# Weight loads two groups ahead instead of three, and sum loads half an interval sooner, in a hybrid attention and linear-attention block on Trainium2

## The chip, the core and the metric

The kernel runs on one core of one Trainium2 chip. The core's engines have queues of their own: TensorE (PE) multiplies matrices, VectorE (DVE) and ScalarE (ACT) work on rows of elements, GpSimd (POOL) helps, and SyncE (SP) issues most DMA transfers. Each queue runs in order. A queue stops at an instruction whose inputs, or whose target buffer, are not ready, and everything behind it stops too.

The metric is the device time of one execution in microseconds (us).

## The reference

The block takes 512 positions of width 2048. It normalises the input, projects it by one wide matrix, sends parts of the result through two token mixers, gates both with SiLU, and projects back:

```python
mod = jax.nn.silu(c) @ w_cond[layer] + b_cond[layer]
shift, scale, gate = jnp.split(mod, 3, axis=-1)
h = rms_norm(x) * (1.0 + scale[:, None]) + shift[:, None]
proj = h @ w_in[layer]
aq, ak, av, ag, gq, gk, gv, gg, lr_f, lr_b = jnp.split(proj, PROJ_SPLITS, axis=-1)
...                      # 16 attention heads over aq, ak, av (three dilated windows)
a_out = att.reshape(B, S, ATT_WIDTH) * jax.nn.silu(ag)
...                      # 4 heads of gated linear attention (GLA) over gq, gk, gv, both directions
g_out = g_o * jax.nn.silu(gg)
y = jnp.concatenate([a_out, g_out], axis=-1) @ w_out[layer]
x = x + gate[:, None] * y
return rms_norm(x) * final_gain
```

Two small products matter here. The row `shift` times the value columns of the weights gives a bias of the values, and `silu(c)` times the last third of `w_cond` gives the output gate. Both are a vector times a matrix, so the kernel doesn't use TensorE for them: VectorE multiplies a block of transposed weights by the row and adds up along it. These are the *sums* of this document.

## The kernel before

**Units.** The wide projection is worked in units of 512 columns: qk2, qk4, qk6, gk, gv0, gv1, ag0, ag1, gg0, gg1 (after two larger stages that don't matter here), and then the output projection. A unit has 8 groups of weights. A group is 256 input rows by 512 columns, 512 KB, loaded by one DMA into a raw buffer. Float32 accuracy comes from splitting: ACT rounds the group to a high part (`split_hi`, L442 in the profile), DVE subtracts that from the raw numbers to get a low part (`split_lo`, L428), and PE makes three products for each one (`three`, L215 to L217). So a group is 24 matmuls of 128x512.

**The ring of raw buffers.** There are four raw buffers of 512 KB (tag `raw`). The groups of weights (named `raw_ag13` for group 3 of unit ag1), the blocks for sums of values (`rawv`) and the blocks for sums of gates (`rawg`) share them. SP issues a load when the buffer's former owner has been read. A value sum (`bias_half`) has a load at L838 and an operation on DVE at L843 or L314; a gate sum (`gate_half`) has its load at L804 and its operation at L314, behind which stands a short read of the accumulator. In the names `rawv40` and `rawg91` the last digit is the half and the rest the number of the column block.

**What runs beside the matmuls.** PE's order is that of the program. In `unit`, after each pair of matmul triples a counter `tick` goes on by one, 64 in all, and side work whose time (a share of the unit) has come is issued there. In qk2 to gk it is attention: per head and window the logits `s` (L730, L731), the maximum and subtraction `p` on DVE (L734), the exponential on ACT, the transposes `t` (L754), their eviction `pt`, the product `o` (L768) and its combination `cat` (L775). In gv1 to gg0 it is GLA, one head per unit: gates `z` (L869) and their decays, `ki` (L898) and its transposes `kt` (L908), states, the masked product `at` (L954), the outputs `go`, their squares `gsq` and `gsl` (L974, L982), a matmul `gn` for the norm (L983, L984), and the normalised result `cat` (L992). Three PSUM banks serve this side work, so that z of the next head waits until L992 of the head before has read its bank.

**What sets the order.** `SUMS_IN` gives the number of sums of each unit (the rest are in gg1). `some_sums` gives each sum q of n two times in the unit: one for its load, (q − 0.3)/n, and one for its operation, (q + 0.7)/n. PE's order follows from the ticks. On the other engines a scheduler sets the order, from the priorities that this order of the program gives and from its own idea of when inputs are there. Gate sums are also held behind the last masking step of GLA (`masked`, L954). Loads of output weights and their combinations on POOL's queue (`T`, L391) are paced by ACT's `split_hi`.

Weights: `unit` fetches, for each group, the groups two and three ahead before it makes the low part of its own; `split_hi` of the next group fetches that, if it isn't fetched yet.

Of the kernel before, what the change touches and what calls it, by code (L numbers as in the profile page):

```python
# [114 lines left out]
SUMS_IN = {"qk6": 4, "gk": 4, "gv0": 9, "gv1": 2, "ag0": 7, "ag1": 9, "gg0": 9}  # L115
# [63 lines left out]
def block_kernel(ctx: ExitStack, tc: tile.TileContext, a: dict):  # L179
# [19 lines left out]
    def PJ(name):  # L199
        return pp.tile([P, 512], F32, tag="pj", bufs=5, name=name)  # L200
# [13 lines left out]
    def three(ps, lh, ll, rh, rl, first, last, more=False):  # L214
        mm(ps, lh, rh, start=first, stop=False, skip_group_check=more)  # L215
        mm(ps, ll, rh, start=False, stop=False, skip_group_check=more)  # L216
        mm(ps, lh, rl, start=False, stop=last, skip_group_check=more)  # L217
# [134 lines left out]
    def fetch(i):  # L352
        if i < len(groups) and i not in raws:
            u, g = groups[i]
            if u == "O":
                raws[i] = out_fetch(g)
            else:
                raws[i] = RAW(f"raw_{u}{g}", [2, 512])
                nc.sync.dma_start(raws[i], a["w_" + u][g])
# [54 lines left out]
    def block_sums(name):  # L414
        n = SUM_OPS_IN[name]
        r = [sum_ops.pop(0) for _ in range(n)]
        return [((q + 0.5) / n, x) for q, x in enumerate(r)]
# [5 lines left out]
    def split_lo(i):  # L423
        if i in raws and i not in low:
            u, g = groups[i]
            raw = raws[i].rearrange("p k c -> p (k c)")
            hi, lo = wts[i]
            tt(lo, raw, hi.bitcast(F32), op=ALU.subtract)  # L428
            low.add(i)

    def split_hi(i):
        if i < len(groups) and i not in wts:
            fetch(i)
            u, g = groups[i]
            raw = raws[i].rearrange("p k c -> p (k c)")
            dst = None
            if (u, g) == ("O", len(groups) - gi["O", 0] - 4):
                t = b8.tile([P, 2, 1024], F32R, tag="b8", name="wlast")
                dst = t[:, 0, :], t[:, 1, :]
            wts[i] = dst or (wp.tile([P, 1024], F32R, tag="whi", name=f"{u}{g}h"),  # L440
                             wp.tile([P, 1024], F32R, tag="wlo", name=f"{u}{g}l"))
            last["hi"] = act(wts[i][0], raw, AF.Copy).ins  # L442
# [177 lines left out]
    n = len(chain) // 2  # L620
# [4 lines left out]
    for z in range(2):  # L625
        for e in range(3):
            name = ("mm", "a", 0, 7) if (z, e) == (1, 2) else ("m0", z, e)
# [224 lines left out]
    def some_sums(name):  # L852
        r = [sum_work.pop(0) for _ in range(SUMS_IN.get(name, len(sum_work)))]
        n = len(r)
        loads = [(max(q - 0.3, 0.1) / n, x[0]) for q, x in enumerate(r)]
        return sorted(loads + [((q + 0.7) / n, x[1]) for q, x in enumerate(r)], key=lambda x: x[0])

    def gla_head(h):
# [142 lines left out]
    def urgent(go):  # L1001
        with tc.high_priority(offset=20):
            go()
# [3 lines left out]
    def unit(name, natural, side=(), lr=None):  # L1007
        side = sorted(spill + list(side) + block_sums(name), key=lambda x: x[0])
        spill[:] = [(at - 1, go) for at, go in side if at >= 1]
        side = [x for x in side if x[0] < 1]  # L1010
        ps = [PJ(f"ps_{name}_{i}") for i in range(4)]
        pos, tick, ticks = 0, 0, 64
        for g in range(KT // 2):
            i0 = gi[name, g]
            split_hi(i0)
            split_hi(i0 + 1)
            for ahead in (2, 3):
                fetch(i0 + ahead)
            split_lo(i0)
            hi, lo = wts[i0]  # L1020
            for i in range(4):
                for kk in range(2):
                    k = 2 * g + kk
                    rh, rl = h_hi[:, k, :], h_lo[:, k, :]
                    if natural:
                        t = slice(i * P, i * P + P)
                        cw = slice(kk * 512, kk * 512 + 512)
                        three(ps[i], rh[:, t], rl[:, t], hi[:, cw], lo[:, cw], k == 0, k == KT - 1)
                    else:
                        c = slice(kk * 512 + i * P, kk * 512 + i * P + P)  # L1030
                        three(ps[i], hi[:, c], lo[:, c], rh, rl, k == 0, k == KT - 1)
                    tick += 1
                    if tick % 8 == 2:
                        split_lo(i0 + 1)
                    while pos < len(side) and side[pos][0] * ticks <= tick:
                        urgent(side[pos][1])
                        pos += 1
                if lr is not None:
                    lr(4 * g + i)
        while pos < len(side):  # L1040
            urgent(side[pos][1])
            pos += 1
        return ps
# [14 lines left out]
    for n, p in (("qk2", 0), ("qk4", 2), ("qk6", 4)):  # L1058
        ps = unit(n, False, attention((p, p + 1)) + ([(0.05, shift_row)] + some_sums(n) if p == 4 else []))
        for q in range(2):  # L1060
            qk_evict(p + 2 + q, ps[2 * q], ps[2 * q + 1])

    ps = unit("gk", False, attention((6, 7)) + some_sums("gk"))
    gla["k"] = B8("gkt", [4, 512])
    for i in range(4):
# [12 lines left out]
    def lr_tick(n):  # L1078
        if n in at_tick:
# [3 lines left out]
            mm(plr[:64], w, h_lo[:, k, :], start=False, stop=k == KT - 1)  # L1083

    ps = unit("gv0", True, some_sums("gv0"), lr=lr_tick)
    gla["v0"] = B8("gv0", [4, 512])
    for i in range(4):
# [340 lines left out]
```

## Time and profile before

| | us |
|---|---|
| median of 3 runs | 942.91 (940.98 to 943.13) |
| the profiled execution | 940.34 |
| its span | 938.6 |
| PE busy in it | 917.5 (98%) |
| DVE busy | 654.6 (70%) |
| ACT busy | 472.2 (50%) |

The profile shows one execution, recorded by the hardware. Its span goes from the first to the last instruction, and times in its rows count from the span's start. A row of a timeline has the start, the duration, the engine, the line of the code, the operation, and the tiles with an arrow from inputs to output; in square brackets stands how long the engine stood idle before it and what ended that. Buffer numbers are left out in the profile's names, so `rawg` stands for all gate blocks. A row of a list of waits has the waiting engine, tile and line, an arrow to what it waited for, and then the sum in us, how many times, and the longest. A row of the list of DMA issues ends with the us from issue to landing. Matmul durations overlap, so their pace is read from start to start. The mean granted clock of TensorE in this execution was 0.994 of the full one.

### The profile page before, as it was taken

The numbers are of one execution on the slowest core, as the hardware profiler recorded it, in microseconds if no ns is written. First come the engines' busy times: TensorE is split into PE (matmuls) and PEld (weight loads), VectorE is DVE, ScalarE is ACT, GpSimd is POOL, SyncE is SP. The second block draws the span as 40 slices with busy tenths as digits, with TensorE's granted clock in tenths as the row PEclk, the third lists the DMA queues.
The fourth block names the chain that finished last, engine by engine and source line by source line (L and its number), as shares of the span: only waits on it lengthen the run. The fifth ranks groups of instructions, "written<-read, shape, count | busy, mean of one in ns | idle before, by whom it ended". The sixth has DMA issues, their size and how long they took to land.

```text
span 938.6 us, 12129 instructions
## 1 busy us (share of the span) xinstructions
PE 917.5 (98%) x4375; PEld 760.8 (81%) x4375; DVE 654.6 (70%) x960; ACT 472.2 (50%) x770; POOL 98.3 (10%) x152
## 2 busy tenths in 40 slices
PE   7999999999999999999999999989989999999996
PEld 6888888888888888888877888878878888888884
DVE  7988899766755676766444657476686639697496
ACT  5553533565655645655413545363643428555464
POOL 0000000012222122122000100111002000000001
PEclk9999999999999999999999999999999999999998
DMA  9999497465765775755656546666766567856743
GB/s 352 404 412 383 166 372 269 158 199 148 188 198 153 217 234 166 239 167 147 209 200 197 162 151 221 202 199 199 247 209 200 187 195 267 315 203 217 276 179 135
DMA packets 54339, 209.79 MB, mean 224 GB/s; under 512 B 7204, under 2 KB 7492, under 8 KB 45960
## 3 DMA queue, kind: packets, MB, share of 16 engines
q1 hardware_dynamic: 48656, 174.83, 51.1%
q0 software_dynamic: 5184, 33.62, 15.1%
q8 instruction: 34, 0.56, 0.2%
q10 hardware_dynamic: 440, 0.57, 0.2%
q14 instruction: 25, 0.20, 0.1%
HBM read 200.53 MB, written 37.83 MB: 254 GB/s over the span
## 4 chain that ended last, share of the span: by engine, by line
PE 81%; DMA 8%; DVE 7%; issue 3%; ACT 1%; POOL 0%; SPq 0%; DVEq 0%; POOLq 0%; ACTq 0%
DMA rawg<-in_wg 5%; PE ps_qk L215 4%; PE ps_qk L217 4%; PE ps_qk L216 4%; PE g L217 4%; PE g L215 4%; PE g L216 4%; PE stb L217 3%; PE stb L216 3%; PE stb L215 3%; PE o L768 3%; PE ps_gv L217 3%; PE ps_gv L216 3%; PE ps_gv L215 3%; PE t L754 3%
## 5 line engine op out<-in xcount | busy, mean ns | idle before, releaser
L737 ACT ACTIVATE p<-p,st 128x512 f32<-128x512 f32 x64 | 46.1, 720 | 56.3 <-DVE st L734 55.9
L314 DVE CUSTOM_DVE_ANT_0 cb<-cb,sb,c_bcond 128x2048 f32<-128x2048 f32 (+1 forms) x32 | 73.4, 2295 | 1.3 <-DMA cb<-in_wm 1.0
L391 POOL DMA_DIRECT2D T<-in_w_o x48 | 33.5, 704 | 311.3 <-ACT qk21h L442 119.8
L742 POOL TENSOR_SCALAR p<-p,st 128x512 f32<-128x512 f32 x62 | 43.2, 697 | 196.1 <-DVE st L738 152.9
L759 DVE TENSOR_TENSOR pt<-t,pt 128x512 fp32r<-128x512 f32 x64 | 43.7, 688 | 15.6 <-ACT pt L758 15.4
L734 DVE CUSTOM_DVE_ANT_0 p<-s,g 128x512 f32<-128x512 f32 x64 | 43.6, 686 | 13.7 <-PE s L731 13.4
L758 ACT ACTIVATE pt<-t 128x512 fp32r<-128x512 f32 x64 | 37.8, 591 | 9.9 <-PE t L754 8.9
L314 DVE CUSTOM_DVE_ANT_0 rawg<-rawg,sb,gate 128x1024 f32<-128x1024 f32 x16 | 20.5, 1283 | 31.1 <-DMA rawg<-in_wg 30.9
L754 PEld LDWEIGHTS t<-c_ident,p 128*128 128x128 f32 x256 | 31.5, 140 | 9.7 <-POOL p L742 1.4
L754 PE MATMUL t<-c_ident,p 128*128 128x128 f32 x256 | 38.5, 273 | 0.1
L768 PEld LDWEIGHTS o<-pt,vv 128*128 128x128 f32 x256 | 34.8, 188 | 2.8
L768 PE MATMUL o<-pt,vv 128*128 128x256 f32 x256 | 35.5, 281 | 0.0
L314 DVE CUSTOM_DVE_ANT_0 rawg<-rawg,sb,c_bcond 128x1024 f32<-128x1024 f32 x16 | 20.5, 1282 | 19.1 <-DMA rawg<-in_wg 19.0
L738 DVE RECIPROCAL st<-st 128x1 f32<-128x1 f32 x64 | 10.3, 161 | 24.9 <-ACT p L737 24.9
L730 PE MATMUL s<-ks,qs 128*128 128x512 f32 x64 | 25.1, 392 | 0.2 <-DVE cat L775 0.2
L731 PE MATMUL s<-kl,qs 128*128 128x512 f32 x64 | 25.0, 391 | 0.0
L937 ACT ACTIVATE sq<-st,sc 128x256 f32<-128x256 f32 x24 | 12.2, 508 | 22.1 <-DVE st L927 13.0
L843 DVE CUSTOM_DVE_ANT_0 rawv<-rawv,shb 128x1024 f32<-128x1024 f32 x8 | 9.8, 1225 | 16.0 <-DMA rawv<-in_wv 16.0
L314 DVE CUSTOM_DVE_ANT_0 rawv<-rawv,shb,vbias 128x1024 f32<-128x1024 f32 x8 | 10.3, 1282 | 15.0 <-DMA rawv<-in_wv 15.0
L1253 POOL TENSOR_SCALAR x<-x,rn 128x512 f32<-128x512 f32 x3 | 3.4, 1137 | 158.4 <-ACT rn L1242 158.4
L771 ACT ACTIVATE oh<-o 64x256 f32<-64x256 f32 x32 | 12.2, 382 | 13.7 <-PE o L768 12.7
L775 DVE TENSOR_TENSOR cat<-o,oh 64x256 f32<-64x256 f32 x32 | 13.3, 416 | 7.6 <-ACT oh L771 7.2
(1520 smaller groups left out, 2978.0 us busy)
## 6 DMA issues: line engine op xcount, KB each, us to landing
cb<-in_wm SPq DMA_DIRECT2D x31, 1024.0 KB, 8.5
T<-in_w_o POOLq DMA_DIRECT2D x48, 512.0 KB, 5.2
rawg<-in_wg SPq DMA_DIRECT2D x32, 512.0 KB, 4.6
raw_O<-T SPq DMA_DIRECT2D x32, 512.0 KB, 5.0
raw_qk<-in_w_qk SPq DMA_DIRECT2D x24, 512.0 KB, 3.3
raw_O<-in_w_o SPq DMA_DIRECT2D x24, 512.0 KB, 4.2
rawb<-in_w_sb SPq DMA_DIRECT2D x16, 512.0 KB, 4.9
T<-T POOLq DMA_DIRECT2D x16, 512.0 KB, 3.6
```

The lines of the kernel that those rows point to most:

```text
L215: mm(ps, lh, rh, start=first, stop=False, skip_group_check=more)
L216: mm(ps, ll, rh, start=False, stop=False, skip_group_check=more)
L217: mm(ps, lh, rl, start=False, stop=last, skip_group_check=more)
L314: nc.vector.tensor_tensor_reduce(out=w, in0=w, in1=with_, op0=ALU.mult, op1=ALU.add, scale=1.0, scalar=init, accum_out=dst)
L391: move = nc.gpsimd.dma_start(dst, src, max_dma_last_dim=8192, **how).ins
L734: nc.vector.tensor_tensor_reduce(out=t, in0=ps, in1=gt[h][:, P * i:P * i + 512], op0=ALU.add, op1=ALU.min, scale=1.0, scalar=3e38, accum_o ...
L737: act(t, t, AF.Exp, bias=st[:, 0:1], scale=-1.0, accum_out=st[:, 1:2])
L742: last["pool"] = nc.gpsimd.tensor_scalar(t, t, st[:, 2:3], 1.0, op0=ALU.mult, op1=ALU.mult).ins
L754: nc.tensor.transpose(pk[:, kt * P:kt * P + P], t[:, kt * P:kt * P + P], ident)
L758: act(hi, src, AF.Copy)
L759: tt(lo, src, hi.bitcast(F32), op=ALU.subtract)
L768: mm(po[:, :256], vv[h // 4][:, kt, h % 4, :], t[:, w, kt, :], start=kt == 0 and w == 0, stop=kt == 3 and w == 1)
```

## The change

In units that have sums (those in `SUMS_IN`, and gg1), `unit` fetches only the group two ahead. In all units, the load of a sum gets the time (q − 0.8)/n in place of (q − 0.3)/n, and at the least 0.05/n in place of 0.1/n; the times of the operations stay.

```diff
--- before.py
+++ after.py
@@ -852,7 +852,7 @@
     def some_sums(name):
         r = [sum_work.pop(0) for _ in range(SUMS_IN.get(name, len(sum_work)))]
         n = len(r)
-        loads = [(max(q - 0.3, 0.1) / n, x[0]) for q, x in enumerate(r)]
+        loads = [(max(q - 0.8, 0.05) / n, x[0]) for q, x in enumerate(r)]
         return sorted(loads + [((q + 0.7) / n, x[1]) for q, x in enumerate(r)], key=lambda x: x[0])
 
     def gla_head(h):
@@ -1014,7 +1014,7 @@
             i0 = gi[name, g]
             split_hi(i0)
             split_hi(i0 + 1)
-            for ahead in (2, 3):
+            for ahead in (2,) if name in SUMS_IN or name == "gg1" else (2, 3):
                 fetch(i0 + ahead)
             split_lo(i0)
             hi, lo = wts[i0]
```

No instruction is added or taken away. PE's and POOL's queues have the same order as before; on SP, DVE and in a few places on ACT the order is another. Three places follow. In all of them a name is the tile's with its number.

First, SP's queue at the end of unit gk, where the value sums of unit gv0 begin. Before:

```order
L359 DMA raw_gv03_4170<-in_w_gv0 128x1024
L838 DMA rawv40_4187<-in_wv 128x1024
L838 DMA rawv41_4202<-in_wv 128x1024
L359 DMA raw_gv04_4219<-in_w_gv0 128x1024
L838 DMA rawv50_4237<-in_wv 128x1024
L1070 DMA lrb_4157<-in_w_lr 128x512
L359 DMA raw_gv05_4252<-in_w_gv0 128x1024
L838 DMA rawv51_4269<-in_wv 128x1024
```

After, from the load of gv02 on:

```order
L359 DMA raw_gv02_4168<-in_w_gv0 128x1024
L838 DMA rawv40_4173<-in_wv 128x1024
L838 DMA rawv41_4191<-in_wv 128x1024
L359 DMA raw_gv03_4217<-in_w_gv0 128x1024
L838 DMA rawv50_4222<-in_wv 128x1024
L838 DMA rawv51_4247<-in_wv 128x1024
L359 DMA raw_gv04_4252<-in_w_gv0 128x1024
L838 DMA rawv60_4281<-in_wv 128x1024
```

The loads of sums 40 and 41 stand ahead of the load of gv03 rather than behind it, and that of sum 50 is right behind the load of gv03, with sum 51's behind it.

Second, DVE's queue at the end of GLA head 1, in unit ag0 and the first groups of ag1. Behind the masking step stand sums 31 and 40, and after the change also 41; then the rows go on. Before:

```order
L428 TENSOR_TENSOR ag10l_5302<-raw_ag10_5194,ag10h_5301 128x1024
L314 ISA rawg41_5289,gate_1489<-rawg41_5289,sb_89,gate0_1490 128x1024
L314 ISA gate_1489 128x1
L974 TENSOR_TENSOR gsq11_5271<-gsq11_5271,gsq10_5258 128x512
L982 TENSOR_TENSOR gsl1_5311<-gsq11_5271,gsh1_5310 128x512
L314 ISA rawg50_5393,gate0_1490<-rawg50_5393,sb_89,c_bcond_84 128x1024
L314 ISA gate0_1490 128x1
L428 TENSOR_TENSOR ag11l_5363<-raw_ag11_5242,ag11h_5362 128x1024
L314 ISA rawg51_5433,gate_1489<-rawg51_5433,sb_89,gate0_1490 128x1024
L314 ISA gate_1489 128x1
L992 TENSOR_SCALAR cat2_4893<-go10_5247,c_ggain_1487,gr1_5316 128x512
```

After:

```order
L428 TENSOR_TENSOR ag10l_5300<-raw_ag10_5242,ag10h_5299 128x1024
L314 ISA rawg50_5368,gate0_1490<-rawg50_5368,sb_89,c_bcond_84 128x1024
L314 ISA gate0_1490 128x1
L974 TENSOR_TENSOR gsq11_5271<-gsq11_5271,gsq10_5258 128x512
L314 ISA rawg51_5420,gate_1489<-rawg51_5420,sb_89,gate0_1490 128x1024
L314 ISA gate_1489 128x1
L982 TENSOR_TENSOR gsl1_5309<-gsq11_5271,gsh1_5308 128x512
L428 TENSOR_TENSOR ag11l_5361<-raw_ag11_5302,ag11h_5360 128x1024
L314 ISA rawg60_5451,gate0_1490<-rawg60_5451,sb_89,c_bcond_84 128x1024
L314 ISA gate0_1490 128x1
L992 TENSOR_SCALAR cat2_4891<-go10_5247,c_ggain_1487,gr1_5314 128x512
```

Ahead of `gsl1`, which PE's `gn` of head 1 needs, there stood one sum behind ag10's low part; now there are two others, 50 and 51, and a third, 41, stands ahead of it. Ahead of L992, for which z of head 2 waits, the last sum was 51 and is 60.

Third, DVE's queue at the same step of head 2, in the first groups of gg0. Before:

```order
L428 TENSOR_TENSOR gg00l_5746<-raw_gg00_5635,gg00h_5745 128x1024
L314 ISA rawg90_5739,gate0_1490<-rawg90_5739,sb_89,c_bcond_84 128x1024
L314 ISA gate0_1490 128x1
L974 TENSOR_TENSOR gsq21_5716<-gsq21_5716,gsq20_5703 128x512
L982 TENSOR_TENSOR gsl2_5755<-gsq21_5716,gsh2_5754 128x512
L314 ISA rawg91_5839,gate_1489<-rawg91_5839,sb_89,gate0_1490 128x1024
L314 ISA gate_1489 128x1
```

After:

```order
L428 TENSOR_TENSOR gg00l_5744<-raw_gg00_5685,gg00h_5743 128x1024
L314 ISA rawg91_5814,gate_1489<-rawg91_5814,sb_89,gate0_1490 128x1024
L314 ISA gate_1489 128x1
L974 TENSOR_TENSOR gsq21_5714<-gsq21_5714,gsq20_5701 128x512
L314 ISA rawg100_5866,gate0_1490<-rawg100_5866,sb_89,c_bcond_84 128x1024
L314 ISA gate0_1490 128x1
L982 TENSOR_TENSOR gsl2_5753<-gsq21_5714,gsh2_5752 128x512
```

Sums 91 and 100 moved ahead of `gsl2`; 90 stands further up. At head 3 one sum, 140, moved ahead of `gsl3` in the same way.

## The prediction

> **What bounds the kernel now.** I read the page's busy times and its chain of waits first, then the list of waits by engine, then the timeline around each wait that stops PE.
>
> ```profile
> PE 917.5 (98%) x4375; PEld 760.8 (81%) x4375; DVE 654.6 (70%) x960; ACT 472.2 (50%) x770; POOL 98.3 (10%) x152
> ...
> PE 81%; DMA 8%; DVE 7%; issue 3%; ACT 1%; POOL 0%; SPq 0%; DVEq 0%; POOLq 0%; ACTq 0%
> DMA rawg<-in_wg 5%; PE ps_qk L215 4%; PE ps_qk L217 4%; PE ps_qk L216 4%; PE g L217 4%; PE g L215 4%; PE g L216 4%; PE stb L217 3%; PE stb L216 3%; PE stb L215 3%; PE o L768 3%; PE ps_gv L217 3%; PE ps_gv L216 3%; PE ps_gv L215 3%; PE t L754 3%
> ```
>
> PE is busy 98% of the span, so matmul time bounds the kernel and the change touches none of it. What can move is PE's few waits. The chain gives 5% to loads of gate weights for sums, `rawg`, although no matmul reads them. PE's waits, then DVE's:
>
> ```profile
> PE kt L908 <- DVE ki L898: 3.1, 1, 3.1
> PE z L869 <- DVE cat L992: 2.9, 1, 2.9
> ...
> PE s L730 <- DVE cat L775: 0.2, 1, 0.2
> PE gn L984 <- DVE gsl L982: 0.2, 1, 0.2
> ```
>
> ```profile
> DVE rawg L314 <- DMA rawg<-in_wg: 50.0, 18, 5.7
> ```
>
> Four waits of PE lie in units with sums, and each is for DVE. DVE in turn stands 50.0 us before `rawg` sums. The two long PE waits and their aftermath on PE's timeline:
>
> ```profile
> 616.29 0.39 PE L216 MATMUL ps_ag<-h_hi,ag10l 128*128 128x512 f32 x1
> 616.52 0.39 PE L217 MATMUL ps_ag<-h_lo,ag10h 128*128 128x512 f32 x1
> 619.81 0.76 PE L869 MATMUL z<-lrst,ups 128*128 128x512 f32 x1 [2.90 <-DVE cat L992]
> 620.37 0.63 PE L215 MATMUL ps_ag<-h_hi,ag10h 128*128 128x512 f32 x1
> ...
> 622.92 0.39 PE L215 MATMUL ps_ag<-h_hi,ag10h 128*128 128x512 f32 x1
> ...
> 641.00 0.49 PE L908 MATMUL kt<-c_ident,ki 128*128 128x128 f32 x3
> ...
> 698.41 0.90 PE L908 MATMUL kt<-c_ident,ki 128*128 128x128 f32 x3 [3.14 <-DVE ki L898]
> ```
>
> Ahead of the wait matmuls start 0.23 us apart (616.29, 616.52). Behind it, from 620.37 to 622.92, six start 0.425 apart. So the z wait costs 2.9 us and about 1.3 of slow matmuls (z and six more, 0.2 each), 4.2 in all. The kt wait costs 3.1 and a slow restart (0.90 for three transposes against 0.49 at 641.00), which I put at 1. With the two waits of 0.2 some 8.7 us, say 9, is the most that this change can win. DVE ahead of the z wait:
>
> ```profile
> 596.14 0.69 DVE L954 SCALAR_TENSOR_TENSOR at<-c_ident,at 128x512 f32<-128x512 f32 x1
> ...
> 601.80 1.28 DVE L314 CUSTOM_DVE_ANT_0 rawg<-rawg,sb,gate 128x1024 f32<-128x1024 f32 x1
> ...
> 606.68 0.69 DVE L982 TENSOR_TENSOR gsl<-gsq,gsh 128x512 fp32r<-128x512 f32 x1 [0.70 <-ACT gsh L981]
> 610.57 1.28 DVE L314 CUSTOM_DVE_ANT_0 rawg<-rawg,sb,c_bcond 128x1024 f32<-128x1024 f32 x1 [3.19 <-DMA rawg<-in_wg]
> ...
> 617.71 1.28 DVE L314 CUSTOM_DVE_ANT_0 rawg<-rawg,sb,gate 128x1024 f32<-128x1024 f32 x1 [4.70 <-DMA rawg<-in_wg]
> 618.92 0.74 DVE L992 SCALAR_TENSOR_TENSOR cat<-go,c_ggain,gr 128x512 f32<-128x512 f32 x1
> ```
>
> L992, which PE wants, stands behind a sum that waits 4.70 us for its load. The load's row on SP's queue, and what loads took here and elsewhere (the first three from 512 KB issues in short windows, the last two over all loads of `rawg` and of `rawv`):
>
> ```profile
> 603.12 9.10 SPq L804 DMA_DIRECT2D rawg<-in_wg  x2
> ```
> ```profile
> rawg<-in_wg SPq DMA_DIRECT2D x1, 512.0 KB, 5.7
> ```
> ```profile
> T<-in_w_o POOLq DMA_DIRECT2D x1, 512.0 KB, 7.7
> ```
> ```profile
> raw_gv<-in_w_gv SPq DMA_DIRECT2D x1, 512.0 KB, 3.1
> ```
> ```profile
> DMA to landing us min/median/max: 3.1/4.6/7.3
> ```
> ```profile
> DMA to landing us min/median/max: 3.3/4.1/5.8
> ```
>
> The second load of the pair goes out at 611.9, when the sum that started at 610.57 has ended: both use the same buffer, since weights three groups ahead hold the other three. Load, sum, load, sum run in series, 5.7 + 1.3 us each.
>
> **The change part by part.** No instruction and no byte is added; PE's and POOL's orders stay. SP issues each sum's load about one place sooner and weights one group later, and DVE's queue gets sums ahead of work that stood before them. The last is what can cost.
>
> *Weights a group later.* A group is 24 matmuls, 5.4 us at 0.227. The closest low part of a unit with gate sums is made 4.3 us before its matmul (start to start):
>
> ```profile
> 739.54 1.22 DVE L428 TENSOR_TENSOR gg12l<-raw_gg,gg12h 128x1024 fp32r<-128x1024 f32 x1
> ```
> ```profile
> 743.88 0.39 PE L216 MATMUL ps_gg<-h_hi,gg12l 128*128 128x512 f32 x1
> ```
>
> Less its 1.22, 3.1 us are left. A later load moves it only where it lands after the place of the split; what now comes ahead of the split on DVE is at most one more sum, 1.28 us. I take 0 and bound it from 0 to 4 us (one load of 7.3 less the lead).
>
> *Value sums, qk6 and gk.* In qk6 the 0.2 us that PE waits for `cat` goes, since the sum ahead of it is loaded sooner: −0.2. At the end of gk the new order puts one more sum, 50, ahead of the attention's `cat` and `p`:
>
> ```profile
> 429.85 0.33 SPq L359 DMA_DIRECT2D raw_gv<-in_w_gv  x1
> 438.61 5.60 SPq L838 DMA_DIRECT2D rawv<-in_wv  x2
> ```
> ```profile
> 442.62 1.23 DVE L843 CUSTOM_DVE_ANT_0 rawv<-rawv,shb 128x1024 f32<-128x1024 f32 x1 [0.50 <-DMA rawv<-in_wv]
> ...
> 446.03 0.69 DVE L734 CUSTOM_DVE_ANT_0 p<-s,g 128x512 f32<-128x512 f32 x1 [0.48 <-PE s L731]
> ```
> ```profile
> 448.87 0.66 PE L754 MATMUL t<-c_ident,p 128*128 128x128 f32 x4
> ```
>
> Sum 40 now loads where gv03 loaded, at 429.85, and 41 follows it in the same buffer. The load of gv03 waits until 41 is done, near 441 by my count (two loads of 4 and two sums from 429.85 on, with DVE's other work between), and SP issues 50's load right behind it, 441.2. With the 4.1 us of the median `rawv` load the sum runs 445.3 to 446.6, and after `cat` (0.42) and its neighbours `p` starts at 447.4 instead of 446.03, so the transposes at 448.87 start about 1.3 late. With a load of 3.3 they are on time, with 5.8 for 50, and 41 late as well, some 3.7 late: **+1.3** (0 to +3.7). At 371 to 376 two sums land alike behind one buffer: 0 (0 to +0.9).
>
> *Gate sums.* The rows on which the rest turns:
>
> ```profile
> 610.15 0.39 PE L984 MATMUL gn<-gsl,ones 128*128 128x512 f32 x1
> ```
> ```profile
> 638.26 0.69 DVE L898 TENSOR_TENSOR ki<-ki,gkt 128x512 f32<-128x512 f32 x1
> ```
> ```profile
> 668.86 0.39 PE L984 MATMUL gn<-gsl,ones 128*128 128x512 f32 x1
> ```
> ```profile
> 697.67 0.68 DVE L898 TENSOR_TENSOR ki<-ki,gkt 128x512 f32<-128x512 f32 x1
> ```
> ```profile
> 724.94 0.68 DVE L982 TENSOR_TENSOR gsl<-gsq,gsh 128x512 fp32r<-128x512 f32 x1
> ...
> 727.77 0.39 PE L984 MATMUL gn<-gsl,ones 128*128 128x512 f32 x1
> ```
>
> Head 1: two buffers now carry sums in turn. Sum 51's load goes out when ag10's split, the operation that ends at 601.80, frees its buffer; at 7.3 us (the slowest `rawg` load; the `T` of this place took 7.7) it lands at 609.1, the sum ends at 610.4, and `gsl`, now behind it, at 611.1: PE's gn is 1.0 late. Sum 60's load goes out at 610.5, takes 5.7 as before, ends with its sum at 617.5, and L992 starts there, 1.4 sooner than 618.92. PE reaches z at 617.8, z can start 0.9 behind L992, 618.4: 0.6 lost, and I take no slow matmuls behind so short a wait. Instead of 4.2, 1.6 is lost: **−2.6**. PE then comes to kt of head 2 at 638.4, where `ki` ended at 638.95 before and has one waiting sum less ahead of it: no new loss.
>
> Head 2 and 3: two sums (91 and 100) stand ahead of `gsl` instead of after it. It ends near 668 (two more sums, 2.6, less the 2.6 by which all is early, from 666.1, with about 2 for loads), while gn is wanted at 666.3: about 1.7 lost. This and the later L992 push `ki` of head 3, whose end at 698.35 sets the kt wait: the way from head 2's mask to kt grows by some 0.8, so 2.6 shrinks to −1.8. Behind it, sum 140 goes ahead of head 3's `gsl`, which has only 2.2 us of slack (725.62 to 727.77): 1.28 of sum and some 2 of waiting for its load, which goes out when sum 131 frees the buffer, make gn 1.2 late (0.2 to 2.4). Gate sums together: **−0.6** (−9 with every load at 3.1 to 3.5; +2 with crowded loads).
>
> A rule to weigh against the z rows: the Trainium skill, "TensorE: Matmul & The Clock Gate", Part 1, has the clock drop to half after an idle window of about 3.4 us. The wait here, 2.9, is shorter and half pace is seen all the same. By the page's figure the slow matmuls would not hang on this wait and the gate sums would come to +0.7; by the row they go with it. The row decides.
>
> Sum: 1.3 − 0.2 − 0.6 = **+0.5 us** on the profiled execution's 940.34, so 940.8. The median of the runs, 942.91, is 2.6 above that execution: **943.4**. A measurement of this kernel tells about 0.3%, 2.8 us, from no change.
>
> **The rivals.**
> *Loads come in bursts (slower).* Sums' loads now start together with weights and with POOL's `T` moves. Where three overlapped, the loads took 5.7 to 7.7 us against 3.1 alone. Decisive is the load of sum 50 near 441: from 5.2 us on it stops PE for more than 2.4. Then the end of gk costs 3.7, heads 10 and 11 cost 0.9, and the gate sums +2: with −0.2 some +6, **949**. Against it: the DMA engines have room at other times, and the number of loads is the same.
> The Trainium skill, "DMA: Bandwidth & Descriptors", section on issuing engines not being separate DMA queues, says that transfers of all engines run on the same 16 DMA engines and interleave. The 7.7 row agrees, and it is this rival's side.
> *Weights become late (slower).* Two groups ahead with 7.3 us loads and an extra sum ahead of each low part use up the 3.1 us: two or three groups of gg0 and gg1 stop PE for 2 to 4, some +8, **951**. For it: leads shrink in just the units with most sums. Against: no row of PE's waits names a weight of any of these units.
> *Serial loads end (faster).* With two buffers in turn, loads land in 3.1 to 4 and sums find their data: PE's waits fall to a third of their 9, −6, and gk's 1.3 stays: −5, **938**. For it: 50.0 us of DVE's waits are of that kind. Against: DVE's new order puts more sums ahead of `gsl`.
> *Nothing comes of it.* The loads start sooner but still each waits for a sum's buffer: **942.9**.
>
> **How the numbers follow.** The forecast's sum has 0.30, no effect 0.04, the faster rival 0.28, bursts 0.26, late weights 0.12. Same is 0.30 + 0.04, slower 0.26 + 0.12. The range leaves out about a tenth on either side: it goes from 937.5, just under the faster case, to 950, between the two slower ones. The likeliest case's own range is 940.1 to 945.7.
>
> **What would show it.** Right: PE's wait at z under 1 us, a new wait of about 1 us for `gsl` at gn of heads 1 to 3, kt of head 3 still waiting for `ki`, and at the end of gk a wait of 1 to 2 us for `p` at L754; DVE's wait for `rawg` falls below 50.0 but not by half. Wrong: any PE wait for a weight's high or low part; the z wait as long as now; or sums' loads with medians above 5.5 us for `rawg`, which would be the bursts.

## The result, and the profile after

The changed kernel takes 946.88 us (median of 5 runs, 945.97 to 949.38) against 942.13 for the kernel before beside it (5 runs, 940.98 to 943.13). The ratio is 1.0055, 95% interval 1.0038 to 1.0072: slower by 0.55%, or 5 us. In a second group of runs (12), on one chip with the last three experiments, it was 1.0045 (1.0024 to 1.0067). Single executions of one kernel differ by several us here, so a difference of 1 or 2 us between two profiles is not told from chance. The one profile of before is of an execution of 940.34 us, while the medians of that kernel beside the experiments lie at 943.19 to 944.37. So a distance to that profile tends to come out too long.

The page of the changed kernel, and its list of PE's waits:

```profile
span 945.1 us, 12135 instructions
PE 919.5 (97%) x4375; PEld 761.0 (81%) x4375; DVE 654.4 (69%) x960; ACT 472.1 (50%) x770; POOL 99.5 (11%) x152
```

```profile
PE kt L908 <- DVE ki L898: 4.2, 2, 2.5
PE t L754 <- DVE st L734: 3.6, 1, 3.6
...
PE gn L983 <- ACT gsh L981: 1.5, 2, 0.8
...
PE gn L984 <- DVE gsl L982: 1.4, 2, 0.8
PE t L754 <- ACT p L740: 0.9, 1, 0.9
```

The 2.9 us at z is gone, as hoped for. In its place stand 2.9 at gn and 4.2 at kt (3.1 before). The largest single wait is a new one, 3.6 us at the transposes `t`, in unit qk6; in the second group's profile of the changed kernel it is there again, with 3.3. The first matmuls of each weight group in both profiles show how the distance between the kernels grows: −0.3 up to qk63; +4.6 at qk64; +5.1 at qk67, the last group of qk6; +6.5 at gv01, after the end of gk; +6.5 at gg04, late in GLA. So most of it is made in qk6, and 4.8 of it at one place: the wait of 3.6, and behind it matmuls at a lower clock (0.51 of the full one from 350.6 to 353.9).

VectorE's timeline in qk6, first before the change, then after. The custom operation on `rawv` with `vbias` in each is the sum of the second half of column block 1, `rawv11`; L734 is the attention step `p` and L759 the eviction `pt`:

```profile
346.00 0.68 DVE L734 CUSTOM_DVE_ANT_0 p<-s,g 128x512 f32<-128x512 f32 x1
346.60 0.08 DVE L734 DVE_READ_ACCUMULATOR2_ANT st<- 128x1 f32 x1
347.28 0.69 DVE L759 TENSOR_TENSOR pt<-t,pt 128x512 fp32r<-128x512 f32 x1 [0.59 <-ACT pt L758]
347.98 0.17 DVE L738 RECIPROCAL st<-st 128x1 f32<-128x1 f32 x1
350.44 1.28 DVE L314 CUSTOM_DVE_ANT_0 rawv<-rawv,shb,vbias 128x1024 f32<-128x1024 f32 x1 [2.30 <-DMA rawv<-in_wv]
```

```profile
341.20 0.67 DVE L759 TENSOR_TENSOR pt<-t,pt 128x512 fp32r<-128x512 f32 x1
341.79 0.40 DVE L775 TENSOR_TENSOR cat<-o,oh 64x256 f32<-64x256 f32 x1
347.38 1.28 DVE L314 CUSTOM_DVE_ANT_0 rawv<-rawv,shb,vbias 128x1024 f32<-128x1024 f32 x1 [5.19 <-DMA rawv<-in_wv]
348.59 0.08 DVE L314 DVE_READ_ACCUMULATOR2_ANT vbias<- 128x1 f32 x1
348.59 0.69 DVE L734 CUSTOM_DVE_ANT_0 p<-s,g 128x512 f32<-128x512 f32 x1
```

The load's issue on SP's queue, and what it took: before (two rows), after (two rows), and POOL's transfer beside it after the change:

```profile
345.07 0.33 SPq L838 DMA_DIRECT2D rawv<-in_wv  x1
```
```profile
rawv<-in_wv SPq DMA_DIRECT2D x1, 512.0 KB, 5.2
```
```profile
339.21 0.33 SPq L838 DMA_DIRECT2D rawv<-in_wv  x1
```
```profile
rawv<-in_wv SPq DMA_DIRECT2D x1, 512.0 KB, 8.0
```
```profile
T<-in_w_o POOLq DMA_DIRECT2D x1, 512.0 KB, 8.7
```

The load starts 5.9 us sooner and lands only 3.1 us sooner, at 347.2 instead of 350.3: it now overlaps most of a transfer of POOL's. The sum's turn on VectorE came forward by more than the landing did. Before, VectorE came to it at 348.1 and waited 2.30; now it comes to it at 342.2 and waits 5.19, and two steps `p` and two evictions `pt`, which used to be done ahead of it, stand behind it. PE's transposes at 349.43 wait for the first of them:

```profile
349.43 0.63 PE L754 MATMUL t<-c_ident,p 128*128 128x128 f32 x4 [3.60 <-DVE st L734]
```

### The profile page after: what moved, and what is told of

It reads as the page before. It is cut to its first block, busy times and chain, and to the rows that moved or that the text cites. A ratio compares the mean times of both kernels' runs of the same rounds, so it can differ in the third digit from the quotient of the medians.

```text
span 945.1 us, 12135 instructions
## 1 busy us (share of the span) xinstructions
PE 919.5 (97%) x4375; PEld 761.0 (81%) x4375; DVE 654.4 (69%) x960; ACT 472.1 (50%) x770; POOL 99.5 (11%) x152
## 4 chain that ended last, share of the span: by engine, by line
PE 79%; DMA 8%; DVE 8%; issue 3%; ACT 2%; SPq 0%; DVEq 0%; POOL 0%; POOLq 0%; ACTq 0%
PE ps_qk L215 4%; PE ps_qk L217 4%; PE ps_qk L216 4%; DMA rawg<-in_wg 4%; PE g L217 4%; PE g L216 4%; PE g L215 4%; DMA rawv<-in_wv 3%; PE stb L217 3%; PE ps_gv L217 3%; PE ps_gv L216 3%; PE ps_gv L215 3%; PE stb L215 3%; PE stb L216 3%; PE o L768 3%
## 5 line engine op out<-in xcount | busy, mean ns | idle before, releaser
L742 POOL TENSOR_SCALAR p<-p,st 128x512 f32<-128x512 f32 x62 | 45.9, 740 | 199.7 <-DVE st L738 157.5
L734 DVE CUSTOM_DVE_ANT_0 p<-s,g 128x512 f32<-128x512 f32 x64 | 43.7, 687 | 15.4 <-PE s L731 15.2
L759 DVE TENSOR_TENSOR pt<-t,pt 128x512 fp32r<-128x512 f32 x64 | 43.7, 688 | 14.2 <-ACT pt L758 13.9
L754 PEld LDWEIGHTS t<-c_ident,p 128*128 128x128 f32 x256 | 31.4, 140 | 14.5 <-issue 4.0
L754 PE MATMUL t<-c_ident,p 128*128 128x128 f32 x256 | 38.5, 273 | 4.6 <-DVE st L734 3.6
L314 DVE CUSTOM_DVE_ANT_0 rawg<-rawg,sb,gate 128x1024 f32<-128x1024 f32 x16 | 20.5, 1284 | 26.1 <-DMA rawg<-in_wg 26.0
L506 ACT ACTIVATE h_hi<-xt,shift 128x512 fp32r<-128x512 f32 x16 | 11.5, 719 | 13.0 <-DVE shift L314 13.0
```

The source lines that it names most:

```text
L314: nc.vector.tensor_tensor_reduce(out=w, in0=w, in1=with_, op0=ALU.mult, op1=ALU.add, scale=1.0, scalar=init, accum_out=dst)
L734: nc.vector.tensor_tensor_reduce(out=t, in0=ps, in1=gt[h][:, P * i:P * i + 512], op0=ALU.add, op1=ALU.min, scale=1.0, scalar=3e38, accum_o ...
L742: last["pool"] = nc.gpsimd.tensor_scalar(t, t, st[:, 2:3], 1.0, op0=ALU.mult, op1=ALU.mult).ins
L754: nc.tensor.transpose(pk[:, kt * P:kt * P + P], t[:, kt * P:kt * P + P], ident)
L759: tt(lo, src, hi.bitcast(F32), op=ALU.subtract)
```

## The experiments

In the theories below, the step "p of window 1" is that of the second block of 128 queries of head 9.

**Each half of the change alone.** First the loads' times:

```diff
-        loads = [(max(q - 0.3, 0.1) / n, x[0]) for q, x in enumerate(r)]
+        loads = [(max(q - 0.8, 0.05) / n, x[0]) for q, x in enumerate(r)]
```

> Sum loads half an interval sooner in all units, weights fetched two and three groups ahead as before the change. Theory A (the loss is made where one sum stands in VectorE's queue ahead of the attention step p of window 1 of head 9, in qk6, while its load is slow; that place needs both parts of the change): here the sum stands behind that p, and value sums at the end of gk are where they were, so the time is within 2 us of before. Theory B (starting the sums' loads sooner crowds the transfers, whatever the weights do): 4 to 6 us above before.

Then the fetches:

```diff
-            for ahead in (2, 3):
+            for ahead in (2,) if name in SUMS_IN or name == "gg1" else (2, 3):
```

> Weights fetched two groups ahead in units with sums, sum loads at their old times. Theory A: in qk6 the sum stands behind the p, so nothing is lost there; the end of gk has the changed kernel's order and costs about 1.4 us; gate sums have nearly the changed kernel's order and come to about zero: 1 to 2.5 us above before. Theory C (fewer weights ahead is what costs): 4 to 6 us above before.

Measured: the loads alone 1.0063 (1.0040 to 1.0087), the fetches alone 1.0078 (1.0053 to 1.0103). Theory A missed in both. The sum did stand behind that `p`, but three operations sooner than before: ahead of both evictions `pt` of head 9 and of the `p` between them. The load went out at 341.9 and 341.5 and took 6.9 and 7.2 us, and PE's product `o` waited for `pt`. The waits of the two kernels, loads alone and then fetches alone:

```profile
PE o L768 <- DVE pt L759: 4.1, 2, 2.6
PE gn L984 <- DVE gsl L982: 2.3, 1, 2.3
```

```profile
PE o L768 <- DVE pt L759: 2.8, 1, 2.8
```

So the place in the queue needs not both halves; each alone moves the sum far enough to lose 2.6 to 3.7 us in qk6. The rest is spread over later units: 2.0 and 1.4 us at the end of gk, 4.2 and 2.1 around gn of head 1, 4.5 around gn of head 2 in the second kernel alone, less the 4.6 that z gives back. Theory B has the size right, and the 4 to 6 us of theory C fall a little short (the medians lie 6.4 apart), but the next runs speak against both.

**The change without qk6, and in qk6 alone.** Both parts, chosen by the unit's name:

```diff
-            for ahead in (2, 3):
+            for ahead in (2,) if name in ('gk', 'gv0', 'gv1', 'ag0', 'ag1', 'gg0', 'gg1') else (2, 3):
```

> Both parts of the change in every unit but qk6. Theory A: the 4.8 us at head 9 are gone, about 0.5 at the start of gk and 1.4 at its end stay, gate sums come to zero: 1.5 to 2.5 us above before. Theory B or C (the loss is spread over units): 4 to 6 us above before.

> Both parts of the change in qk6 only. Theory A: TensorE waits 3 to 4 us for p at the same matmul, 4 to 5.5 us above before. Theory B or C: one unit in nine, under 1.5 us above before.

Measured: without qk6 0.9962 (0.9943 to 0.9982), in qk6 alone 1.0070 (1.0042 to 1.0098). One unit of the eight that have sums (the expectation says nine) makes all of the loss, and the same change elsewhere makes the kernel faster by 0.4%, some 4 us. Theory A had the place right and the gain of the rest wrong: it expected 1.5 to 2.5 us above before. The wait with the change in qk6 alone is the changed kernel's:

```profile
PE t L754 <- DVE st L734: 3.5, 1, 3.5
```

**The sum's place against the load's time.** The changed kernel, with the sum `rawv11` held on VectorE behind the eviction `pt` of head 9's first block. In the trace it then stands behind that of the second block too, as before the change. Its load goes out as early as in the changed kernel:

```diff
-                tt(lo, src, hi.bitcast(F32), op=ALU.subtract)
+                steps[h, i] = tt(lo, src, hi.bitcast(F32), op=ALU.subtract).ins
...
-                cond_sum(vbias[:, m:m + 1], raw, shb[0][:, 1024:], vbias0[:, m:m + 1])
+                with tc.issue_after(steps[9, 0]) if m == 1 else nullcontext():
+                    cond_sum(vbias[:, m:m + 1], raw, shb[0][:, 1024:], vbias0[:, m:m + 1])
```

> The changed kernel, with the second sum of column block 1 (rawv11) held on VectorE's queue behind the first eviction pt of head 9, where it stood before the change; its load still starts early. Theory D (the loss in qk6 is made by the sum's place in VectorE's queue, not by the load's time): the 4.8 us there are gone, the rest of the change stays, 2 to 5 us below before as the run without qk6 was. Theory B (the early load itself costs): still 3 us or more above before.

Measured: 0.9979 (0.9952 to 1.0005), and against the changed kernel's 1.0055 and 1.0045 the loss is gone. The load is as slow as in the changed kernel, yet VectorE doesn't wait for it, and PE has no wait in qk6:

```profile
rawv<-in_wv SPq DMA_DIRECT2D x1, 512.0 KB, 7.7
```
```profile
345.18 0.68 DVE L736 CUSTOM_DVE_ANT_0 p<-s,g 128x512 f32<-128x512 f32 x1
...
346.47 0.69 DVE L761 TENSOR_TENSOR pt<-t,pt 128x512 fp32r<-128x512 f32 x1 [0.59 <-ACT pt L760]
347.07 1.28 DVE L314 CUSTOM_DVE_ANT_0 rawv<-rawv,shb,vbias 128x1024 f32<-128x1024 f32 x1
```

(The lines are two further down in this kernel.) This bears out theory D: no cost of the early load can be told; the early place of its sum is what costs. The sum even finds its data, so the 2.30 us that VectorE waited before are gone; what that is worth in time no run shows.

**The transfer beside it.** The changed kernel without POOL's transfer T1 of block 3:

```diff
-            paced(dsum[pair, name, g], flat(out_block(pair, OUT_SUMS[name][1], g)), accum_op=ALU.add)
+            if (pair, name, g) != (0, "T1", 3):
+                paced(dsum[pair, name, g], flat(out_block(pair, OUT_SUMS[name][1], g)), accum_op=ALU.add)
```

> The changed kernel without one of POOL's transfers, the second part of the output-weight combination T1 of block 3, which lies beside rawv11's load (so the output of this kernel leaves that part out). Theory E (the load is slow because it overlaps that transfer): rawv11's load takes 4.0 to 5.5 us instead of 8.0, TensorE's wait for p at head 9 falls from 3.6 to under 1.5, the time is 0 to 2 us from before. Against it (the load is slow from the transfers of SP's own queue): it stays at 7 or more and the wait at 3 or more.

Measured: 1.0003 (0.9974 to 1.0031). The load and the two waits for it, of VectorE and of PE:

```profile
rawv<-in_wv SPq DMA_DIRECT2D x1, 512.0 KB, 5.1
```
```profile
344.00 1.28 DVE L314 CUSTOM_DVE_ANT_0 rawv<-rawv,shb,vbias 128x1024 f32<-128x1024 f32 x1 [2.27 <-DMA rawv<-in_wv]
```
```profile
PE t L755 <- DVE st L735: 0.7, 1, 0.7
```

Theory E holds: one transfer of another queue makes 2.9 of the 8.0 us, and with it gone PE waits 0.7 instead of 3.6. So the loss takes both, the early place of the sum and the slow load; without either of them it is gone. The Trainium skill, "DMA: Bandwidth & Descriptors", section on issuing engines not being separate DMA queues, says that transfers started by any engine run on the same 16 DMA engines and interleave; 8.0 against 5.1 agrees. The same page of the Trainium skill, section "Rules for kernel authors", tells to issue a load early and to wait for it late. The run with the hold shows what the second half is worth: early with a late wait, PE lost nothing in qk6; early with an early wait, it lost 4.8 us.

**The gate sums alone.** The change in gv1, ag0, ag1, gg0 and gg1 only:

```diff
+        back, least = (0.8, 0.05) if name in ('gv1', 'ag0', 'ag1', 'gg0', 'gg1') else (0.3, 0.1)
+        loads = [(max(q - back, least) / n, x[0]) for q, x in enumerate(r)]
...
+            for ahead in (2,) if name in ('gv1', 'ag0', 'ag1', 'gg0', 'gg1') else (2, 3):
```

> Both parts of the change in gv1, ag0, ag1, gg0 and gg1 only. By the run without qk6, whose end of gk lost 1.5 us: that 1.5 is gone, and the gate sums give the same, so 4 to 6 us below before. If the gain of that run hangs on value sums that are done sooner: 0 to 2 below.

Measured: 0.9978 (0.9954 to 1.0002), some 2 us below before, nearer to the smaller of the two expectations and no better than the run without qk6 (0.9962, intervals overlapping). The 1.5 us at the end of gk, which the profiles had shown, did not come back: this kernel has before's order of work there, and its profile still comes to gv00 1.8 us later than the one profile of before, 1.2 of it at the end of gk. That loss can't be told from the spread of executions.

Its waits show what is left in GLA:

```profile
PE kt L909 <- DVE ki L899: 3.4, 3, 2.5
PE gn L985 <- DVE gsl L983: 2.4, 2, 1.8
...
PE gn L984 <- ACT gsh L982: 0.9, 1, 0.9
```

**Sums kept behind `gsl`.** To that kernel, one line:

```diff
-            tt(lo, sq, hi.bitcast(F32), op=ALU.subtract)
+            masked.append(tt(lo, sq, hi.bitcast(F32), op=ALU.subtract).ins)
```

> As the run with the change in gv1 to gg1 only, and every gate sum that is issued after a head's norm is held behind that head's gsl, so that no waiting sum stands between the squares and gsl. If sums ahead of gsl cost the 1 to 2 us that TensorE waits at gn: these waits go, and it is 1 to 3 us below that run. If the held sums only wait later: TensorE waits as long at kt or z, and it is no faster.

Measured: 0.9952 (0.9926 to 0.9977), by the medians 3.1 us below the kernel without that line, 937.70 against 940.80 on one chip. Again in the last group:

> The change in gv1 to gg1 with the gsl hold once more: 4 to 8 us below before, no wait of TensorE at gn.

There it was 0.9956 (0.9941 to 0.9972), 938.78 us against 943.19. PE waits neither at gn nor at z, and VectorE's wait for `rawg` falls to about half of the 50.0 us before (26.1 and 31.3). Both lists of the first of the two runs:

```profile
PE kt L909 <- DVE ki L899: 3.7, 2, 1.9
```

```profile
DVE rawg L314 <- DMA rawg<-in_wg: 26.1, 12, 6.0
```

The loads of `rawg` are no faster there. For them the list says, for this kernel, then for the changed one:

```profile
DMA to landing us min/median/max: 3.1/5.3/7.8
```

```profile
DMA to landing us min/median/max: 3.0/4.5/8.1
```

The hold without the early loads, on the kernel before, was not run. So it is not shown how much of this gain needs the change at all.

**Both holds on the full change.** `rawv11` behind `pt`, gate sums behind `gsl`:

> The changed kernel with both holds: rawv11 behind the first eviction pt of head 9, and gate sums behind each head's gsl. If the two losses were independent (the sum's place in qk6, sums ahead of gsl): 4 to 9 us below before, near the run with the change in gv1 to gg1 and the gsl hold, plus up to 1.5 us for the end of gk. If the two early stages' loads disturb later ones: no better than the run with the first hold alone, 2 us below before.

Measured: 0.9965 (0.9946 to 0.9983), some 3 to 4 us below before: faster, and faster than the changed kernel beside it, but just short of the 4 to 9 that independent losses would give, and no better than the change in GLA alone with its hold.

**Sums kept behind `ki` as well.**

```diff
-                tt(ki, ki, gk, op=ALU.mult)
+                early = tt(ki, ki, gk, op=ALU.mult).ins
+                if d == 1 and h:
+                    masked.append(early)
```

> As the run with the change in gv1 to gg1 and the gsl hold, and the sums of a unit also held behind the key step ki of the backward direction (heads 1 to 3). If the waits at kt come from sums ahead of ki: they go, 1 to 4 us below that run. If held sums keep raw buffers and so make weights late: TensorE waits for low parts of weights, and it is slower than that run.

Measured: 0.9943 (0.9923 to 0.9963), 936.96 us against 943.19, the fastest kernel of all; its interval overlaps that of the kernel without this hold, so no more than a tie with it is shown. Both expectations came in part: its list of PE's waits has no kt, but half a us for a weight, and a new wait at the masked product for the states, which now have sums ahead of them on VectorE:

```profile
PE att L950 <- DVE st L935: 3.3, 2, 2.6
...
PE ps_gg L216 <- DVE gg04l L428: 0.5, 1, 0.5
```

## Where the prediction was right and where it was wrong

The measured 946.88 lies in the range of 937.5 to 950. The likeliest case, no change that can be told, was wrong: the kernel is slower by more than 0.3%, for which the chance stood at 0.38.

- **The step that failed: the value sums of qk6 at −0.2.** It measured +4.8 at head 9 in the profile (+5.4 in all of qk6), and the change in qk6 alone makes 1.0070. I had seen that the sum's load goes out sooner, and so had the wait go. I took the gain of the earlier load and didn't ask what would be beside it, nor how far the sum itself would move in VectorE's queue. Both were to be had: in the timeline before, `T` goes out at 337.28, and the order of the changed kernel has `rawv11` ahead of the step `p` of head 9's second block.
- **The rival of bursts** had the mechanism, loads of 5.2 us and more beside POOL's `T` with attention steps queued behind the sum, and 949. Its place was wrong. It named sum 50 at the end of gk (+3.7), and it struck at sum 11 in qk6 with 8.0 us. Its +2 for the gate sums didn't come either.
- **The end of gk, +1.3.** The profile shows +1.4, with the wait at L754 for `p` that I had named (0.9). But the kernels with the change in GLA alone and in qk6 alone, with before's order there, show 1.2 and 1.6, against the one profile of before. The term is not confirmed.
- **Gate sums, −0.6.** From the second group of gv0 to the fifth of gg0 the two profiles keep their distance (0.0). By its parts: z was to keep 0.6 and keeps nothing; gn of head 1 was to lose 1.0 and loses 1.9, because sum 50's load took 7.4 beside a `T` of 8.3 and held even the squares; kt of head 2 was to lose nothing and loses 1.9; gn of head 2 1.9 for 1.7; gn of head 3 nothing for 1.2. Gn of head 0 gives back 0.8 and kt of head 3 0.5. That the sum comes out near is luck: parts that are off by up to 1.9 cancel. The runs add what the profile couldn't tell: by themselves gate sums make the kernel some 2 us faster (0.9978, an interval that just reaches 1).
- **Weights a group later, 0.** Right: no wait of PE in the changed kernel's list is for a weight's part. The rival of late weights, 951, is out.
- **What would show it.** The z wait is under 1, gn of heads 1 and 2 waits, and so does kt of head 3: right. The wait for `p` at the end of gk, 0.9, is just under the 1 to 2 named. A wait of VectorE for `rawg` between half and all of 50.0: right, 45.8. Gn of head 3: wrong. The median of `rawg` loads stayed (4.5 after 4.6), so by my own sign the bursts were ruled out, and yet one burst decided it. A median was the wrong sign for a loss made by one load.

## What to carry to other kernels

An earlier load is worth no more than it lands earlier, and the scheduler may move the load's user forward too: here it put the sum where VectorE then stood 5.19 us for the data. On an in-order queue the user's place then decides, more than the load's time: look, for each waiting operation that the change moves, at what stands right behind it and which transfers of all queues are in flight. Tying the users of early loads behind the steps that TensorE waits for turned the full change from a loss of 0.5% (1.0045) into a gain of 0.35% (0.9965), and raised the gain of the change in GLA alone from 0.2% to about 0.5%.

## What the runs showed of the hardware

One 512 KB load in qk6 took 5.1 us without and 8.0 us with another queue's transfer beside it. Issued at 339.2, 341.9 (loads alone) and 345.1 (before), it took 8.0, 6.9 and 5.2 us: 5.9 us of issue time became 3.1 us of landing time, 347.2 to 350.3.

How long TensorE stood idle does not tell by itself what comes behind. In the changed kernel, behind a wait of 2.46 us at kt of head 3, matmuls start 0.42 to 0.43 us apart:

```profile
704.74 0.55 PE L908 MATMUL kt<-c_ident,ki 128*128 128x128 f32 x3 [2.46 <-DVE ki L898]
...
707.59 0.63 PE L216 MATMUL ps_gg<-h_hi,gg03l 128*128 128x512 f32 x1
708.01 0.63 PE L217 MATMUL ps_gg<-h_lo,gg03h 128*128 128x512 f32 x1
708.44 0.63 PE L215 MATMUL ps_gg<-h_hi,gg03h 128*128 128x512 f32 x1
```

With `rawv11` held, behind a wait of the same length at the same place, they are soon 0.23 apart:

```profile
699.01 0.55 PE L911 MATMUL kt<-c_ident,ki 128*128 128x128 f32 x3 [2.46 <-DVE ki L901]
...
700.93 0.40 PE L216 MATMUL ps_gg<-h_hi,gg03l 128*128 128x512 f32 x1
701.16 0.40 PE L217 MATMUL ps_gg<-h_lo,gg03h 128*128 128x512 f32 x1
701.40 0.39 PE L215 MATMUL ps_gg<-h_hi,gg03h 128*128 128x512 f32 x1
```

The granted clock in the 3.3 us behind the wait was 0.65 in the first and 1.00 in the second, and the way from kt to the first matmul of gg04 took 4.69 and 3.08 us. Behind the wait of 2.81 us at `o` in the run with the fetches alone the clock was 1.00 as well; behind those of 2.90 and 3.14 us in the kernel before it was 0.52 and 0.58. Behind the wait of 3.60 us in qk6 matmuls ran at full pace for 1.2 us, and only then did the clock fall to 0.51. In the run with the gate sums alone two waits of 0.88 and 0.64 us, at gn of head 2, were enough: from 671.3 to 674.6 matmuls start up to 0.43 apart.

The Trainium skill, "TensorE: Matmul & The Clock Gate", Part 1, gives about 3.4 us of idling before the clock halves; here 2.46 us was once enough and once not. So the rule weighed in the prediction is not a lower bound, and a wait of 2.46 us cost little beyond its own time in one kernel and 1.6 us more in the other.
